# Gated product of 8192 x 8192 in fp32: four-row groups in three 64 KiB slots, products packed in place, stores of 64 KiB a partition

## The chip, the core and the metric

The kernel runs on one core of a Trainium2 chip. The core has a scalar engine (ACT), a vector engine (DVE), a sync engine (SP) that here only issues transfers, GpSimd (POOL), and 16 DMA engines that move data between the chip's memory (HBM) and the core's on-chip buffer (SBUF, 128 partitions). The metric is device time in microseconds (us), lower is better. Time before: 933.41 us, the median of three runs (933.37 to 933.46).

## The reference

The input is one fp32 matrix of 8192 rows and 8192 columns. The left half of each row is multiplied by the sigmoid of the right half:

```
def reference(x):
    a, b = np.split(x, 2, axis=-1)
    return a * (1 / (1 + np.exp(-b)))
```

So 268.4 MB are read, 134.2 MB are written, and each output element costs one sigmoid and one product.

## The kernel before

The rows are cut into 32 tiles of 256 rows. In a tile each of the 128 partitions holds two whole rows that follow each other in HBM: 64 KiB of input (`x_sb`, two slots) and 32 KiB of output (`o_sb`, two slots). A tile's input is one contiguous stretch of 8 MiB in HBM, its output one of 4 MiB.

For each tile `_tiles` records, in program order:

- L58, one load on SP's queue into the tile's input slot. It waits for the product that last read the slot, that is of two tiles before.
- L76, the sigmoid on ACT, in place over the right halves (one instruction of 128x8192 for both rows).
- L77, the product on DVE, from the input slot into the output slot.
- L70, one store on ACT's queue, which waits for the product.

The first tile and the last have four quarter instructions of 128x2048 instead of the one sigmoid and the one product, and the last tile's output goes out in four stores of 1 MiB, each when its quarter is done. The engines run their own instructions in order, and a DMA instruction that has to wait holds up what is behind it on its engine. The framework's automatic dependencies are reduced by hand (`implied`) to the ones that are needed.

L43 is a transfer that computes nothing. It goes out first on ACT's queue and reads 15 pieces of 64 bytes for each of 16 partitions into the tile `idle`, which nothing uses. Its packets stand in ACT's queue ahead of the first store's.

`_launch_early` moves the first load ahead of the start-up barrier, so that it is issued at time 0. `_close_on_sync` rewrites the closing: POOL waits for all transfers but the last and clears the semaphores, and SP waits for the last store. Both functions are left as they are.

A DMA is cut into one packet for each contiguous run of a partition: a load is 128 packets of 64 KiB, a store 128 packets of 32 KiB, so each of the 16 DMA engines gets 8 packets of it, and a 4-byte one that counts up the semaphore. Loads stand in SP's queue (q1 in the profile) and stores in ACT's (q10); the same 16 engines serve both.

Of the kernel before, what the change touches and what calls it, by code (L numbers as in the profile page):

```python
# [8 lines left out]
def _tiles(ctx, tc, x, out):  # L9

    nc = tc.nc
    P = nc.NUM_PARTITIONS  # L20
    DEP = mybir.DependencyInfo(mybir.DependencyClass.Sync, mybir.DependencyReason.DATA)
    fp32 = mybir.dt.float32
    SIG = mybir.ActivationFunctionType.Sigmoid

    n_rows, n_cols = x.shape
    half = n_cols // 2
    R = 2
    SLOTS = 2
    n_tiles = n_rows // (P * R)
    x_t = x.rearrange("(n p r) m -> n p (r m)", p=P, r=R)  # L30
    out_t = out.rearrange("(n p r) m -> n p (r m)", p=P, r=R)

    pool = ctx.enter_context(tc.tile_pool(name="io", bufs=1))
    xs = [pool.tile([P, R * n_cols], fp32, name=f"x_sb{k}") for k in range(SLOTS)]
    os = [pool.tile([P, R * half], fp32, name=f"o_sb{k}") for k in range(SLOTS)]

    def implied(later, *earlier):
        for e in earlier:
            tc.declare_no_dep(later.ins, e.ins, reason="follows from the waits that are kept")

    KEEP = 15
    idle = pool.tile([16, KEEP * 32], fp32, name="idle")
    held = nc.scalar.dma_start(  # L43
        out=idle.rearrange("p (k m) -> p k m", m=32)[:, :, 0:16],
        in_=x[0:16, 0 : KEEP * P].rearrange("p (k m) -> p k m", m=P)[:, :, 0:16],
    )
    tc.keep_in_program_order(held)

    gone = [{k: [] for k in ("loads", "sigs", "muls", "stores")} for _ in range(SLOTS)]
    last_stores = [[] for _ in range(SLOTS)]  # L50
    for i in range(n_tiles):
        old = gone[i % SLOTS]
        freed = last_stores[i % SLOTS]
        now = {k: [] for k in old}
        rows = xs[i % SLOTS].rearrange("p (r h m) -> p r h m", r=R, h=2)
        packed = os[i % SLOTS].rearrange("p (r m) -> p r m", r=R)

        load = nc.sync.dma_start(out=xs[i % SLOTS], in_=x_t[i])  # L58
        implied(load, *old["loads"], *old["sigs"])
        now["loads"].append(load)  # L60

        if 0 < i < n_tiles - 1:
            parts = [(slice(0, R), slice(0, half))]
        else:
            w = half // 2
            parts = [
                (slice(r, r + 1), slice(c * w, (c + 1) * w)) for r in range(R) for c in range(2)
            ]
        def store(cols):
            ins = nc.scalar.dma_start(out=out_t[i, :, cols], in_=os[i % SLOTS][:, cols])  # L70
            now["stores"].append(ins)

        chunks = []
        for k, (r, c) in enumerate(parts):
            b = rows[:, r, 1, c]
            sig = nc.scalar.activation(out=b, in_=b, func=SIG)  # L76
            mul = nc.vector.tensor_mul(out=packed[:, r, c], in0=rows[:, r, 0, c], in1=b)  # L77
            implied(sig, *old["sigs"], *old["muls"], *old["loads"])
            implied(mul, *old["muls"], *old["loads"], *now["loads"])
            by_sigmoid = i % 2 == 1 and len(parts) == 1  # L80
            implied(mul, *(s for s in old["stores"] if by_sigmoid or s not in freed))
            if by_sigmoid:
                for s in freed:
                    tc.add_manual_dep(sig.ins, s.ins.name, DEP, reason="frees the output slot")
            tc.keep_in_program_order(sig)
            now["sigs"].append(sig)
            now["muls"].append(mul)
            chunks.append(slice(r.start * half + c.start, r.start * half + c.stop))
            if i == n_tiles - 1 and k > 0:
                store(chunks[k - 1])  # L90
        store(chunks[-1] if i == n_tiles - 1 else slice(0, R * half))
        for s in now["stores"]:
            implied(s, *old["loads"], *old["sigs"], *old["muls"], *now["loads"], *now["sigs"])
        for k in old:
            old[k] += now[k]
        last_stores[i % SLOTS] = now["stores"]


def _launch_early(nc):
# [68 lines left out]
@with_exitstack  # L168
def kernel(
    ctx: ExitStack,  # L170
    tc: tile.TileContext,
    x: bass.AP,
    out: bass.AP,
):
    nc = tc.nc
    with ExitStack() as pools:
        _tiles(pools, tc, x, out)
    tc.close()
    tc.compile()
    _launch_early(nc)  # L180
    _close_on_sync(nc)
# [30 lines left out]
```

## Time and profile before

| | |
|---|---|
| median of the runs | 933.41 us |
| span of the profiled execution, first to last instruction | 931.87 us |
| median less span | 1.54 us |
| bytes moved | 402.68 MB, 432 GB/s over the span |
| DVE busy | 278.6 us (30%), 38 products |
| ACT busy | 227.0 us (24%), 38 sigmoids |
| sigmoid, 128x8192 and 128x2048 | 7029 and 1901 ns |
| product, 128x8192 and 128x2048 | 8692 and 2287 ns |
| load, issue to landing (median) | 42.2 us |
| store of 4 MiB, issue to landing (median) | 42.0 us |

The profile was taken from one execution. Its own time is the span of 931.87 us and what lies around it, which the runs put at 1.54 us. An engine's busy share says how much of the span it worked. The share of a DMA queue is the time that its packets took, over 16 engines and the whole span, so the shares of the queues add up to how busy the DMA engines were. The trace also has a record of every packet (queue, size, start, duration).

### The profile page before, as it was taken

How to read it: one execution, taken by the hardware profiler on the slowest of the kernel's cores; microseconds unless marked ns; L12 is line 12 of the kernel's file. 1: busy time of each engine (PE TensorE's matmuls, PEld its weight loads, DVE VectorE, ACT ScalarE, POOL GpSimd, SP SyncE). 2: the span in 40 equal slices, each digit the busy share in tenths (PEclk: the TensorE clock that was granted, in tenths of full speed). 3: DMA queues.
4: the chain of work that ended last, by engine and by line, in shares of the span. 5: the costliest groups of instructions: out<-in, count | busy, mean ns of one | idle time of the engine just before them, and what ended most of it. 6: DMA issues, size and time to landing. Idle time of an engine off the chain costs nothing.

```text
span 931.9 us, 249 instructions
## 1 busy us (share of the span) xinstructions
DVE 278.6 (30%) x38; ACT 227.0 (24%) x39; POOL 0.2 (0%) x4
## 2 busy tenths in 40 slices
DVE  0333312333123331133321333213332133321333
ACT  1413332133320333202332023320233202333023
POOL 0000000000000000000000000000000000000000
DMA  9999999999999999999999999999999999999999
GB/s 405 448 408 430 447 428 450 411 464 408 428 450 428 450 409 466 408 428 450 428 450 408 464 411 428 450 425 453 405 459 419 428 450 425 453 405 453 425 428 405
DMA packets 9905, 402.68 MB, mean 432 GB/s; under 512 B 1328, under 2 KB 1328, under 8 KB 1328
## 3 DMA queue, kind: packets, MB, share of 16 engines
q1 hardware_dynamic: 4608, 268.44, 66.6%
q10 hardware_dynamic: 5296, 134.24, 33.4%
q14 instruction: 1, 0.01, 0.0%
HBM read 268.45 MB, written 134.22 MB: 432 GB/s over the span
## 4 chain that ended last, share of the span: by engine, by line
DMA 72%; DVE 15%; ACT 12%; issue 0%; ACTq 0%
DMA x_sb<-in_x_dram 72%; DVE o_sb L77 15%; ACT x_sb L76 12%; ACTq L70 0%; ACTq L76 0%
## 5 line engine op out<-in xcount | busy, mean ns | idle before, releaser
L77 DVE TENSOR_TENSOR o_sb<-x_sb 128x8192 f32<-128x8192 f32 (+1 forms) x38 | 278.6, 7344 | 645.0 <-ACT x_sb L76 645.0
L76 ACT ACTIVATE x_sb<-x_sb 128x8192 f32<-128x8192 f32 (+1 forms) x38 | 225.7, 5950 | 693.2 <-DMA x_sb<-in_x_dram 691.9
L76 ACT ACT_TABLE_LOAD x1 | 1.3, 1283 | 1.2 <-PEq L196 1.2
L196 POOL MEMSET const-bfloat16-1.0<- 128x1 bf16 x1 | 0.1, 102 | 0.0
L196 POOL MEMSET const-uint8-127<- 128x1 uint8 x1 | 0.1, 101 | 0.0
L196 POOL MEMSET const-float32-0.0<- 128x1 f32 x1 | 0.1, 100 | 0.2 <-issue 0.2
L196 POOL MEMSET const-float32-1.0<- 128x1 f32 x1 | 0.1, 98 | 0.0
## 6 DMA issues: line engine op xcount, KB each, us to landing
out_dram<-o_sb ACTq DMA_DIRECT2D x31, 4096.0 KB, 42.0
out_dram<-o_sb ACTq DMA_DIRECT2D x4, 1024.0 KB, 7.9
x_sb<-in_x_dram SPq DMA_DIRECT2D x32, 42.2
idle<-in_x_dram ACTq DMA_DIRECT2D x1, 15.0 KB, 41.4
```

The source lines that it names most:

```text
L76: sig = nc.scalar.activation(out=b, in_=b, func=SIG)
L77: mul = nc.vector.tensor_mul(out=packed[:, r, c], in0=rows[:, r, 0, c], in1=b)
L196: nc = _bacc.Bacc("TRN2", target_bir_lowering=False, num_devices=1)
```

## The change

The tile becomes a group of 512 rows: each partition holds four rows that follow each other in HBM. A group has two halves of two rows, each loaded by one DMA of 8 MiB (L54 of the changed kernel), so that a partition's 64 KiB runs now lie 128 KiB apart in HBM. There are three slots of 64 KiB a partition and no output slots: the first half of a group goes to slot 0 or 2 in turn, the second half always to slot 1.

All sigmoids (L67) and products (L71) are half-row instructions of 128x2048, eight for each group. The products are packed in place: those of all four rows go, one behind the other, into the slot of the group's first half, over input that has been read. Three sigmoids of a group wait for the earlier product whose input lies where the following product will write: quarter 2 for product 0, quarter 3 for product 1, and the first of the second half for product 3.

A group's output goes out in one store of 64 KiB a partition, 8 MiB (L78). Exceptions: the first row of the first group is stored at once (16 KiB a partition) and its other three rows together (48 KiB); the last group goes out in two stores of 16 KiB a partition and four of 8 KiB.

The load of the next group's second half waits for the last product of this group, which frees slot 1. The load of the first half two groups on waits for this group's whole store to land, which frees its slot. Both stand on SP's queue in this order. The first load is cut in two (a row each, 32 KiB a partition), and the first four loads wait for nothing. The transfer into `idle` is gone.

There are 33 loads and 22 stores, where there were 32 loads, 35 stores and the transfer into `idle`. The core of the diff:

```
-    R = 2
-    SLOTS = 2
...
-    held = nc.scalar.dma_start(
-        out=idle.rearrange("p (k m) -> p k m", m=32)[:, :, 0:16],
-        in_=x[0:16, 0 : KEEP * P].rearrange("p (k m) -> p k m", m=P)[:, :, 0:16],
-    )
...
-        load = nc.sync.dma_start(out=xs[i % SLOTS], in_=x_t[i])
...
-            sig = nc.scalar.activation(out=b, in_=b, func=SIG)
-            mul = nc.vector.tensor_mul(out=packed[:, r, c], in0=rows[:, r, 0, c], in1=b)
...
+    R, H = 2, 2
+    n_groups = n_rows // (P * R * H)
+    x_t = x.rearrange("(g p h r) m -> g h p (r m)", p=P, h=H, r=R)
+    out_t = out.rearrange("(g p q) m -> g p (q m)", p=P, q=H * R)
+    slots = [pool.tile([P, R * n_cols], fp32, name=f"x_sb{k}") for k in range(3)]
+    def slot(g, h):
+        return 1 if h else 2 * (g % 2)
...
+    def load(g, h, needs=(), parts=1):
+        width = R * n_cols // parts
+        k = slot(g, h)
+        for j in range(parts):
+            c = slice(j * width, (j + 1) * width)
+            ins = place([k], nc.sync.dma_start(out=slots[k][:, c], in_=x_t[g, h][:, c]), *needs)
...
+    def work(g, h, k):
+        r, c = k // 2, k % 2 * quarter
+        of, to = slot(g, h), slot(g, 0)
+        a = slots[of][:, r * n_cols + c : r * n_cols + c + quarter]
+        b = slots[of][:, r * n_cols + half + c : r * n_cols + half + c + quarter]
+        at = (h * R + r) * half + c
+        before = {(0, 2): (g, 0, 0), (0, 3): (g, 0, 1), (1, 0): (g, 0, 3)}
+        over = [mul_of[m] for m in [before.get((h, k))] if m]
+        sig = nc.scalar.activation(out=b, in_=b, func=SIG)
+        place([of], sig, load_of[g, h, r], *over)
...
+        mul = nc.vector.tensor_mul(out=slots[to][:, at : at + quarter], in0=a, in1=b)
+        mul_of[g, h, k] = place(sorted({of, to}), mul, sig)
+    def store(g, lo, hi, done):
+        c = slice(lo * quarter, hi * quarter)
+        k = slot(g, 0)
+        ins = place([k], nc.scalar.dma_start(out=out_t[g][:, c], in_=slots[k][:, c]), done)
+        store_of.setdefault(g, []).append(ins)
+    load(0, 0, parts=2)
+    load(0, 1)
+    load(1, 0)
+    for g in range(n_groups):
+        first, final = g == 0, g == n_groups - 1
+        for k in range(4):
+            work(g, 0, k)
+            if first and k == 1:
+                store(g, 0, 2, mul_of[g, 0, 1])
+        if final:
+            store(g, 0, 2, mul_of[g, 0, 1])
+            store(g, 2, 4, mul_of[g, 0, 3])
+        for k in range(4):
+            work(g, 1, k)
+            if final and k > 0:
+                store(g, 3 + k, 4 + k, mul_of[g, 1, k - 1])
+        if final:
+            store(g, 7, 8, mul_of[g, 1, 3])
+            break
+        load(g + 1, 1, [mul_of[g, 1, 3]])
+        store(g, 2 if first else 0, 8, mul_of[g, 1, 3])
+        if g + 2 < n_groups:
+            load(g + 2, 0, store_of[g])
```

`place` keeps of the automatic dependencies only those that are named, and keeps the program order.

More of the change, by code (lines that the diff above doesn't have):

```diff
@@ L26, in _tiles @@
     half = n_cols // 2
-    R = 2
-    SLOTS = 2
-    n_tiles = n_rows // (P * R)
-    x_t = x.rearrange("(n p r) m -> n p (r m)", p=P, r=R)
-    out_t = out.rearrange("(n p r) m -> n p (r m)", p=P, r=R)
-    pool = ctx.enter_context(tc.tile_pool(name="io", bufs=1))
[L34 to L39, printed above, removed]
@@ L41, in _tiles @@
-    KEEP = 15
-    idle = pool.tile([16, KEEP * 32], fp32, name="idle")
-    held = nc.scalar.dma_start(
-        out=idle.rearrange("p (k m) -> p k m", m=32)[:, :, 0:16],
-        in_=x[0:16, 0 : KEEP * P].rearrange("p (k m) -> p k m", m=P)[:, :, 0:16],
-    )
[L47 to L96, printed above, removed]
@@ new lines, in _tiles @@
+    quarter = half // 2
+    R, H = 2, 2
+    n_groups = n_rows // (P * R * H)
+    x_t = x.rearrange("(g p h r) m -> g h p (r m)", p=P, h=H, r=R)
+    out_t = out.rearrange("(g p q) m -> g p (q m)", p=P, q=H * R)
+    pool = ctx.enter_context(tc.tile_pool(name="io", bufs=1))
+    slots = [pool.tile([P, R * n_cols], fp32, name=f"x_sb{k}") for k in range(3)]
+    traced = [[] for _ in slots]
+    load_of, mul_of, store_of = {}, {}, {}
+    def slot(g, h):
+        return 1 if h else 2 * (g % 2)
@@ new lines, in place @@
+    def place(touched, ins, *needs):
+        kept = {n.ins.name for n in needs}
+        seen = set()
+        for k in touched:
+            for e in traced[k]:
+                if e.ins.name not in kept | seen:
+                    seen.add(e.ins.name)
+                    tc.declare_no_dep(ins.ins, e.ins, reason="follows from the waits that are kept")
+            traced[k].append(ins)
+        tc.keep_in_program_order(ins)
+        return ins
+    def load(g, h, needs=(), parts=1):
[4 more added lines that the diff above has]
+            ins = place([k], nc.sync.dma_start(out=slots[k][:, c], in_=x_t[g, h][:, c]), *needs)
+            for r in range(R) if parts == 1 else [j]:
+                load_of[g, h, r] = ins
@@ new lines, in work @@
+    def work(g, h, k):
[8 more added lines that the diff above has]
+        place([of], sig, load_of[g, h, r], *over)
+        for m in over:
+            tc.add_manual_dep(sig.ins, m.ins.name, DEP, reason="read before the product goes over it")
+        mul = nc.vector.tensor_mul(out=slots[to][:, at : at + quarter], in0=a, in1=b)
+        mul_of[g, h, k] = place(sorted({of, to}), mul, sig)
```

## The prediction

> **What bounds the kernel now.** I read the page first: the slices, then the shares of the DMA queues.
>
> ```profile
> span 931.9 us, 249 instructions
> ...
> DVE 278.6 (30%) x38; ACT 227.0 (24%) x39; POOL 0.2 (0%) x4
> ...
> DMA  9999999999999999999999999999999999999999
> ...
> q1 hardware_dynamic: 4608, 268.44, 66.6%
> q10 hardware_dynamic: 5296, 134.24, 33.4%
> ```
>
> Loads (q1) and stores (q10) fill 66.6 + 33.4 = 100.0% of 16 DMA engines over the span. No slice is under 9. So the DMA engines set the end, and the chain of waits, which gives ACT and DVE 26%, misleads: its pieces lie beside transfers of other tiles. Next, the DMA view of one pair of tiles, 41.2 to 99.2 us:
>
> ```profile
> DMA packets 576, 25.17 MB, mean 434 GB/s; under 512 B 64, under 2 KB 64, under 8 KB 64
> ...
> q1 hardware_dynamic: 288, 16.78, 66.7%
> q10 hardware_dynamic: 288, 8.39, 33.5%
> ```
>
> Of 288 packets 256 carry data. A 64 KiB packet took 0.667 x 58 x 16 / 256 = 2.418 us, a 32 KiB one 0.335 x 58 x 16 / 256 = 1.215 us; the trace's packet records say 2.418 and 1.213. They alternate strictly, one load packet, one store packet, whatever their size. Two small packets cost 2 x 1.213 - 2.418 = 8 ns more than a large one, and neighbours in the records overlap by about 4 ns, so a packet costs 4 to 8 ns beside its bytes. Change of DMA costs two 4-byte records, 6 ns each: a tile takes 29.00 us, and 8 x (2.414 + 1.2097) = 28.99. **Time can go away only as packets, or as gaps of the DMA engines; it can come only as gaps or slower packets.** Gaps today: 1.0 us before the first packet, 0.6 us more in it, and one at 38 to 41 us. One engine's records there (start, queue and bytes, ns):
>
> ```
> 35.700 L65536 2453
> 38.149 S64 11
> 38.156 L65536 3095
> 41.248 S4 9
> 41.254 L4 9
> 41.260 S32768 1213
> ```
>
> The load packet took 3.095 us in place of 2.45, and so on all 16 engines: 0.65 us at the first store's start, behind the transfer into `idle`.
>
> **The change, part by part.**
>
> *Packets.* For each DMA engine: before 256 load and 248 + 32 store packets = 536. After: loads 31 x 8 + 2 x 8 = 264, stores 22 x 8 = 176, together 440. 96 fewer, at 4 to 8 ns: -0.4 to -0.8, I take -0.5 us (nearer to the period of 29.00, which holds the 4). DMAs with their 4-byte packet: 68 to 55, 13 x 6 ns = -0.1 us.
>
> *The transfer into `idle`.* 15 packets of 11 ns (about 7 after the overlap) = -0.1 us, and six load packets beside them that took 2.453 instead of 2.418: -0.2 us. The gap of 0.65 us: it goes if it belongs to this transfer's end, and stays if it belongs to the first store as such. I take it as gone, because a ring that wakes up in the middle of load packets cost nothing in the one other place (the first 64-byte packet at 6.50 stands behind a load packet of 2.418). Ends 0 and -0.65.
>
> *Sigmoids and products.* After, 128 of 128x2048 each: ACT 128 x 1.9 = 243 us, DVE 128 x 2.285 = 292 us, 14 more than now. All of it lies beside transfers: eight products are 18.3 us of a group's 24 x 2.414 = 57.94. Costed at nothing while the loads queued are enough to cover it; what it costs otherwise is rival 1. In place or in another tile, I give a product the same time; no row shows the difference.
>
> *Waits.* The wait for products 0, 1 and 3 holds sigmoids 2 and 3 of a first half by some 0.5 us and 0.1 us; behind them stand only sigmoids that are not late. Dangerous are the two loads on SP. Count from B, the end of a group's last load packet. Landing to ACT: 1.08 us (41.25 to 42.33). Four sigmoids and products:
>
> ```profile
> 22.03 7.31 ACT L76 ACTIVATE x_sb<-x_sb 128x2048 f32<-128x2048 f32 x4 [19.54 <-DMA x_sb<-in_x_dram]
> 23.97 8.89 DVE L77 TENSOR_TENSOR o_sb<-x_sb 128x2048 f32<-128x2048 f32 x4 [23.97 <-ACT x_sb L76]
> 32.89 25.55 SPq L58 DMA_DIRECT2D x_sb<-in_x_dram  x2
> 32.90 0.37 ACTq L70 DMA_DIRECT2D out_dram<-o_sb  x1
> ```
>
> These lines are before's first tile: the sigmoids' start at 22.03, the end of the products at 23.97 + 8.89 = 32.86, both issues at once. So store and next load are issued at B + 1.08 + 10.83 + 0.03 = B + 11.95. Issue to first packet: 1.0 to 1.6 us on empty queues (the first load), at most 4.1 under way (the store issued at 916.86 follows at 920.93 without a gap). I take 1.3: ready at B + 13.25. Meanwhile the other half-group's load runs in packets of 2.414. When the transfer into `idle` was issued, at 0.78, the packet running and one more came first; so here packet 6 and packet 7, and the store starts at 7 x 2.414 = B + 16.90. Eight alternations, 1:1 now: its last packet ends at 16.90 + 15 x 2.414 = B + 53.11, lands 0.83 later (70.25 to 71.08 for before's first store), and the load that waits for it on SP is ready at 53.11 + 0.83 + 0.05 + 1.3 = B + 55.3. The loads queued by then last until 24 x 2.414 = B + 57.94. **Margin 2.6 us, no gap.** Nothing else stands behind that load on SP. ACT waits for the store's product with the next group's sigmoids behind, whose load lands at about B + 23: late for nobody.
>
> *Ends.* At the start 24 MiB of loads are queued without a wait (58 us of transfers), and the first row's store goes in between: they last until 1.6 + 24 x 2.414 + 8 x 0.606 = 64.4, and the first group's last product is due at 45.1 + 11.95 = 57.1. At the end the store packets left when the loads stop last 14 x 0.606 = 8.5 us, and the first quarter's store is ready at 1.08 + 1.91 + 2.29 + 1.3 = 6.6; further quarters come every 2.2 us, each with 8 x 0.306 = 2.45 us of packets. No gap, as now (912 to 931: store packets all the way).
>
> *Sum.* -0.5 - 0.1 - 0.3 - 0.65 = -1.55 us against the execution's 931.87 + 1.54 = 933.41, which is also the median. **931.9 us**; with the gap at the first store 932.5, with the packets at 8 ns and all gone 931.5.
>
> **Two rules of the Trainium skill, weighed.** The trace shows loads whose runs lie 64 KiB apart at 2.418 us a packet, and no run at 128 KiB. "DMA: Bandwidth & Descriptors", section "Latency and other measured facts", tells of copies that lose with the run's pitch: at 512 KiB 207 GB/s of 214 that are full, at 2 MiB 164. By its 3%, which it gives for four times this pitch, the loads' 619 us would grow by an estimated 20 us; below that pitch it has no row, and I add nothing. The trace shows the change from one DMA to the next at 12 ns. [...]
>
> **Rivals.**
>
> 1. *The load queue runs dry once in a group: slower.* The load two groups on waits for the whole 8 MiB store, where before it waited for a product. For it: the margin is one packet. If issue to first packet takes over 14.48 - 11.95 = 2.5 us in mid-stream (the rows allow 1.0 to 4.1), the store slips by a packet, its last one ends at B + 55.52, at 2.6 us the load is ready at 55.52 + 0.88 + 2.6 = 59.0, 1.07 us late, and each gap also costs 0.6 us of refilling, as in the first packet. A gap makes the next group earlier against its loads, so every second group has one: 7 x (1.07 + 0.6) = 11.7 us at 2.6, 7 x (2.57 + 0.6) = 22 at 4.1, and then smaller gaps in the other groups too. 943 to 959, most likely 944. Against: the first load's 1.0 to 1.6.
> 2. *Each waking of the store queue costs the 0.65 us seen at 41 us: slower.* Before, stores stand in q10 without a break; now it is empty for 57.94 - 36.2 = 22 us in each group. 15 x 0.65 = 9.8 us: 941.6. Against: the waking at 6.50.
> 3. *Reads at 128 KiB pitch are slower.* Each 1% on a load packet is 6.2 us; below, nothing to gain, as the load packets ran at one speed throughout. No bound from a row above; at 1 to 2% 938 to 944.
> 4. *The stores' 64 KiB runs go out as two packets of 32 KiB*: 120 packets come back, +0.6: 932.5, no change.
>
> **How the numbers follow.** Forecast 0.65, its own range 931.4 to 932.8; rival 1 0.20; rival 2 0.07; rival 3 0.06; rival 4 0.02. A measurement of this kernel tells 0.2% (1.9 us) from no change, so faster begins under 931.5: only the forecast with every term at its good end, and something more at the start or end, 0.12. Within 0.2%: 0.53 + 0.02 = 0.55. Slower: 0.33. The range takes in the forecast, rivals 2 and 4, and the nearer halves of rivals 1 and 3: 931.3 to 945.0, which leaves out some 0.16 (rival 1 above 945 about 0.09, rival 3 0.02, below 931.3 0.05).
>
> **What would show it.** Right: both DMA queues' shares add up to 100% again; 4224 data packets in q1 and 2816 in q10, 2.418 us at 64 KiB for both; a period of 57.94 us from group to group; the load two groups on issued about 2.6 us plus 1.3 before its first packet; no long packet at the first store. Rival 1: DMA slices under 9 at 58 or 116 us steps, a store that starts at B + 19.3. Rival 2: one load packet of about 3.1 us at each store's start. Rival 3: load packets over 2.43 us throughout. The forecast is wrong if the sum of the shares falls under 99.5%.

## The result and the profile after

The changed kernel takes **947.58 us** (median; 945.78 to 951.10), the kernel before 933.39 us in the same comparison: a ratio of **1.0156, 95% interval 1.0144 to 1.0168**. The forecast was 931.9, with a range of 931.3 to 945.0. The profiled execution took 945.78 us, its span is 944.4 us, 12.5 more than before's 931.87. The page of after:

```profile
span 944.4 us, 374 instructions
...
DVE 284.9 (30%) x128; ACT 238.8 (25%) x129; POOL 0.2 (0%) x4
...
DMA  9999999999999999999999999999999999999998
...
q1 hardware_dynamic: 4752, 268.44, 66.8%
q10 hardware_dynamic: 3168, 134.22, 32.8%
q14 instruction: 2, 0.02, 0.0%
```

The packets are the forecast ones: 4752 less 528 of 4 bytes are 4224 in q1, 3168 less 352 are 2816 in q10. The DMA row is full and the shares still add up to 99.6%. So by the page alone nothing seems lost, and yet the same bytes took 12.5 us longer. A share counts the time that a packet is under way, and a packet that stalls in the middle counts as busy. What shows the loss is the rate. Stretches of 58 us (columns: stretch, its length, busy time of DVE, ACT and POOL, clock, DMA share, GB/s), before:

```profile
110.00:168.00 58.00, 17.41 (x3) 14.06 (x2) 0.00 (x0) 1.00 1.00 434
...
748.00:806.00 58.00, 17.39 (x3) 14.06 (x2) 0.00 (x0) 1.00 1.00 434
```

and after:

```profile
110.00:168.00 58.00, 17.68 (x9) 14.84 (x8) 0.00 (x0) 1.00 1.00 434
...
342.00:400.00 58.00, 16.58 (x8) 14.84 (x8) 0.00 (x0) 1.00 1.00 432
400.00:458.00 58.00, 17.06 (x9) 14.65 (x8) 0.00 (x0) 1.00 1.00 417
458.00:516.00 58.00, 15.24 (x8) 12.29 (x8) 0.00 (x0) 1.00 1.00 428
516.00:574.00 58.00, 17.24 (x8) 14.29 (x9) 0.00 (x0) 1.00 0.99 421
...
748.00:806.00 58.00, 17.80 (x8) 13.76 (x8) 0.00 (x0) 1.00 1.01 424
```

At first after runs at before's 434 GB/s, up to 400 us at 432; then it falls to between 417 and 428 with the share still at about 1.00. The issues of the stores say the same: 110.94, 169.06, 227.14, 285.20 (58.06 to 58.12 apart), then 58.6 to 60.5 apart.

How the packets lie is seen in the DMA view of two such stretches, each cut into 40 slices of 1.45 us; a packet's bytes count where it starts. First 110 to 168 us, then 748 to 806 us of after:

```profile
GB/s 226 497 723 0 723 226 497 723 0 723 226 497 723 0 723 271 452 723 0 723 271 452 723 0 723 316 407 723 0 723 316 407 723 0 723 316 407 723 0 723
```

```profile
GB/s 633 226 588 316 407 633 226 588 271 362 90 588 316 542 316 407 588 316 542 316 407 588 316 542 316 407 588 316 542 316 407 588 316 542 316 407 588 316 452 407
```

In the first stretch the 16 DMA engines go in step: in some slices all of them start a packet (723), and in every fifth none does (0). In the second there is no empty slice left: some engines stand a part of a packet or a whole one behind the others. I call the time between the first and the last engine at the same packet their **spread**. Before, it is 0.5 to 0.7 us from end to end; in after, at the last packet of each store, it is 0.4 at the start, 1.5 at 325 us and 2 to 4 from 380 us on.

In the packet records the loss can be summed up, as time over the usual length of a packet (2.418 us at 64 KiB), mean of 16 engines: load packets lose 11.8 us in after (before 1.5, all in the first 42 us), store packets 0.1, idle time is 4.4 us (before 1.7). That is 10.3 + 2.7 more, and less the 0.5 us of packets saved the 12.5 us of the spans. Of the 11.8 us 9.5 lie in one kind of load: the first half of a group, which waits for a whole store. (The records do not name the engine. Where a reading below goes by engine, I chained them by start and end; between engines that stand a whole packet apart this can swap two.)

### The profile page after: what moved, and what is told of

It is laid out like the page before. It is cut to its first block, busy times and chain, and to the rows that moved or that the text cites. A ratio compares the mean times of both kernels' runs of the same rounds, so it can differ in the third digit from the quotient of the medians.

```text
span 944.4 us, 374 instructions
## 1 busy us (share of the span) xinstructions
DVE 284.9 (30%) x128; ACT 238.8 (25%) x129; POOL 0.2 (0%) x4
## 3 DMA queue, kind: packets, MB, share of 16 engines
q1 hardware_dynamic: 4752, 268.44, 66.8%
q10 hardware_dynamic: 3168, 134.22, 32.8%
## 4 chain that ended last, share of the span: by engine, by line
DMA 81%; DVE 15%; ACT 3%; issue 0%; ACTq 0%; SPq 0%
DMA x_sb<-in_x_dram 81%; DVE x_sb L71 15%; ACT x_sb L67 3%; ACTq L78 0%; SPq L54 0%; ACTq L67 0%
## 5 line engine op out<-in xcount | busy, mean ns | idle before, releaser
L71 DVE TENSOR_TENSOR x_sb<-x_sb 128x2048 f32<-128x2048 f32 x128 | 284.9, 2287 | 652.3 <-ACT x_sb L67 652.3
L67 ACT ACTIVATE x_sb<-x_sb 128x2048 f32<-128x2048 f32 x128 | 237.5, 1901 | 695.3 <-DMA x_sb<-in_x_dram 681.3
```

Of the source, the lines that this page charges most:

```text
L71: mul = nc.vector.tensor_mul(out=slots[to][:, at : at + quarter], in0=a, in1=b)
```

## The experiments

The theories have letters, where an expectation does not say itself what one stands for. Where only one time is given, the kernel ran once. A and B put the loss on the loads by themselves (A on the 128 KiB from run to run), G on each waking of the store queue (a store that starts after the queue was empty), D on the thin margin of the load that waits for a store, D' on an instruction fetch that makes a DMA engine late, E on 64 KiB store packets beside 64 KiB load packets by themselves, D2 on the wait of a load for the whole store, with engines that stand apart.

### Loads and their pitch

**e1**: after, with each load's rows in one stretch (64 KiB from run to run).

```
-    x_t = x.rearrange("(g p h r) m -> g h p (r m)", p=P, h=H, r=R)
+    x_t = x.rearrange("(g h p r) m -> g h p (r m)", p=P, h=H, r=R)
```

> The changed kernel with one edit: each load reads one contiguous 8 MiB again, so a partition's 64 KiB runs lie 64 KiB apart instead of 128 KiB; slots, waits, packets and stores are those of the changed kernel. (The rows then reach the output in another order than the reference's; the work is the same.) Theory A, the load packets are slow because of the 128 KiB pitch, in the stretches where loads run alone: 931.9 to 932.6 us, load packets back at 2.418 us. Theory B, load packets are slow wherever loads run alone in the middle of the run, whatever their pitch: 945 to 951 us as for the changed kernel. Theory C, the waking of the store queue costs it: 945 us too, with the long packets only at the stores' starts.

Measured: 944.38 us (941.38 to 948.15), ratio 1.0131 (1.0096 to 1.0166). The loss stays, and starts at the same place.

**e2**: before, with after's pitch.

```
-    x_t = x.rearrange("(n p r) m -> n p (r m)", p=P, r=R)
+    x_t = x.rearrange("(g p h r) m -> g h p (r m)", p=P, h=2, r=R)
...
-        load = nc.sync.dma_start(out=xs[i % SLOTS], in_=x_t[i])
+        load = nc.sync.dma_start(out=xs[i % SLOTS], in_=x_t[i // 2, i % 2])
```

> The kernel before with one edit: the loads' runs lie 128 KiB apart (rows again reach the output in another order), nothing else. Here a load packet always alternates with a store packet, except in the first 41 us. Theory A as I hold it (the pitch hurts where loads run alone at 434 GB/s of reads): only the first 41 us and nothing or little after, 933.4 to 935 us. A stronger theory A (the pitch hurts everywhere): 3% on the load packets, 945 us or more. Theories B and C: 933.4 us.

Measured: 933.25 us (933.20 to 933.39), ratio 0.9999 (0.9990 to 1.0008). **r1** and **r2** make the 32 loads alone, at either pitch, and one store at the end:

```
+    for i in range(n_groups * H):
+        nc.sync.dma_start(out=xs[i % 3], in_=x_t[i // H, i % H])
+    nc.scalar.dma_start(out=out_t[0], in_=xs[i % 3][:, 0 : R * half])
```

> Loads alone: the 32 loads of 8 MiB into three slots in turn and one store at the end; no sigmoid, no product, no other store (left out). Runs 64 KiB apart. 256 packets of 2.414 us for each DMA engine are 618 us, some 622 with the start and the end. Theory A: 622 us. Theory B: the same 3% as in the lone stretches of the changed kernel (10.4 us in some 350), 635 us or more.

> Loads alone as in the run with 64 KiB, but runs 128 KiB apart. Theory A: 635 us or more, with load packets of 2.5 us and over in the mean. Theory B: the same time as with 64 KiB, both slow. Theory C: 622 us, no slow packets, as no store starts.

Measured: 636.28 and 636.27 us; the loads end at 622.09 us in both, and the last store, which I had left out of the sum, takes the rest. No long load packet after the first. Pages of r1 and r2:

```profile
span 634.5 us, 79 instructions
...
q1 hardware_dynamic: 4608, 268.44, 97.8%
```

```profile
span 634.5 us, 79 instructions
...
q1 hardware_dynamic: 4608, 268.44, 97.9%
```

The span and the time of a packet are the same at both pitches, so A and B fall. The Trainium skill, "DMA: Bandwidth & Descriptors", section "Latency and other measured facts", has a loss at 512 KiB of pitch and more, in copies between tensors in HBM; at the 128 KiB of these loads the ratio of 0.9999 shows none.

### Wakings, the transfer into `idle`, the fetch

**e6**: before without L41 to L48, the transfer into `idle`.

> The kernel before without the transfer into idle, nothing else. The sum of the prediction gave -0.3 us for its packets and -0.65 us for the gap at the first store. The changed kernel has no such transfer and still shows a gap of 0.7 us at its second store, so I now expect the gap to stay: 933.0 us. If the gap was the transfer's: 932.4 us. If the transfer keeps the store queue behind the loads, so that the last tile's products are covered by store packets: a gap at the end, 935 us or more.

Measured: 933.19 us against 933.40, ratio 0.9998 (0.9989 to 1.0007). The long load packet at the first store is still there (0.88 to 1.11 us over). It belongs to the first store, and after has it too (0.26 us at 21 us and 0.70 at 57).

**g0** runs before with quarter instructions for all tiles, as a base; **g2** and **g4** are g0 with only every second or every fourth tile stored:

```
-        if 0 < i < n_tiles - 1:
+        if False:
...
-        store(chunks[-1] if i == n_tiles - 1 else slice(0, R * half))
+        if i % 2 == 0 or i == n_tiles - 1:
+            store(chunks[-1] if i == n_tiles - 1 else slice(0, R * half))
```

> Control for the next two: the kernel before with every tile in quarter instructions on ACT and DVE (as the first and the last tile are), stores and loads as they were. ACT has as many sigmoids as the changed kernel and should fetch instructions at some 350 us too. Theory D' (a fetch in the middle starts the trouble in any schedule): long load packets after it, 938 us or more. Theory G (trouble needs a store queue that runs empty and wakes up beside loads alone): 933.4 us, nothing after the fetch.

> As the control, but only every second tile (and the last) is stored; the other outputs are left out. Store packets stay 32 KiB, no load waits for a store, and a load's margin is 19.3 - 13.3 = 6 us, so the load queue cannot run dry by a wait. Store packets alternate with loads half of the time, then the loads run alone for 19 us and the next store wakes the queue, 15 times. Clean sum for a DMA engine: 256 x 2.414 + 128 x 1.21 + 32 x 0.306 = 782.6, with start, end and the 1.5 us outside some 788 us. Theory D (the trouble is the load that waits for a store): 788 us. Theory G (each waking can cost 0.3 to 1.8 us, as seen in the changed kernel after 336 us): 795 us or more, long load packets just ahead of the stores' first packets.

> As the last one with every fourth tile stored: 7 to 8 wakings, each after loads alone for some 58 us. Clean sum 256 x 2.414 + 64 x 1.21 + 32 x 0.306 = 705.2, some 710.5 us in all. Theory D: 710.5 us. Theory G: 714 us or more, with as much or more for each waking as with every second store.

Measured: g0 933.87, g2 788.52, g4 711.62 us, the two latter 0.5 and 1.1 over their clean sums of 788 and 710.5. After the first store a waking costs 0.00 to 0.01 us, so a waking by itself costs nothing, and G falls. In g0 the fetch of ACT's instructions, at 289 and 366 us, put one engine back and cost nothing.

**e3a** and **e3b** move that fetch (after has it at 336.4 and 338.9 us): the first half of a group in row instructions, or its quarters in four pieces.

```
-        mul = nc.vector.tensor_mul(out=slots[to][:, at : at + quarter], in0=a, in1=b)
+        mul = nc.vector.tensor_mul(out=slots[to][:, at : at + n], in0=a, in1=b)
...
+        cut = 4 if h == 0 else 1
+        for j in range(cut):
+            p = slice(j * w, (j + 1) * w)
```

> The changed kernel with the first half of each group in two row instructions (128x4096) in place of four quarters on ACT and DVE; the second half, on which the store waits, is left. ACT has some 9 instructions a group instead of 11, so its 63rd, where the fetch came at 336 us, falls at some 400 us. Theory D: the schedule is clean until then, the long load packets start after the fetch, 938 to 948 us. Theory E: they start at about 336 us as before.

> The changed kernel with the first half's quarters cut into four pieces of 128x512 each on ACT and DVE: 16 instructions in place of four, in time that is not on the path. ACT reaches its 63rd instruction in the third group. Theory D: the fetch comes at 130 to 180 us, and further fetches follow; long load packets from then on, 945 to 960 us. Theory E: they start at about 336 us.

Measured: 958.59 and 948.60 us. In e3a the fetch comes at 462 us, but the engines split at the very first store and the loss begins at 99 us; in e3b fetches come from 119 us on and the loss begins at 215. e3a is slower than D had it, and neither loss starts at 336 us, as E had it. The fetch is one thing that moves engines apart, and not needed. D' falls.

### The wait of a load for a store

**e5** widens the margin, by 5 us on paper: the second half is loaded by rows, each as soon as its row is free.

```
-            ins = place([k], nc.sync.dma_start(out=slots[k][:, c], in_=x_t[g, h][:, c]), *needs)
+            ins = place([k], nc.sync.dma_start(out=slots[k][:, c], in_=x_t[g, h][:, c]), *(needs if parts == 1 else needs[j : j + 1]))
...
-        load(g + 1, 1, [mul_of[g, 1, 3]])
+        load(g + 1, 1, [mul_of[g, 1, 1], mul_of[g, 1, 3]], parts=2)
```

> The changed kernel, but the load of a group's second half is two DMAs, one row each (32 KiB packets), each waiting for the products that read its row. The stores stay one of 64 KiB a partition, the first half's load still waits for the whole store. The last two quarters alone are left to do when the last load packet lands: the store is issued at B + 1.08 + 6.44 = B + 7.5 instead of B + 11.95, so it ends two packets earlier and the margin of the load behind it grows from 2.6 to some 7.5 us. Theory D (the margin of one packet is used up when one DMA engine falls behind, first by the fetch of ACT's instructions at 336 us; from then the load queues of the others run dry in each group): 932.3 to 933.5 us, some 0.6 of it for 8 more packets a group, and no long load packets after 336 us. Theory E (64 KiB stores alternating 1:1 with loads drive the engines apart by themselves): 940 us or more.

Measured: 949.48 us (946.17 to 955.03), ratio 1.0172 (1.0125 to 1.0219). No better, so a thin margin is not the whole cause. The loss has another form: the spread at the stores' last packets grows to 3 to 7 us, one engine is late at a time, load packets lose 7.7 us and store packets as much (in after 0.1), and 4.9 of the 6.3 us of idle time lie at the end. The loads that wait for a store lose at most 0.5 us each.

**e4** makes two stores of 32 KiB a partition out of each store; the slot's next load waits for both.

```
-            store(g, 2, 4, mul_of[g, 0, 3])
+        store(g, 2 if first or final else 0, 4, mul_of[g, 0, 3])
...
-        store(g, 2 if first else 0, 8, mul_of[g, 1, 3])
+        store(g, 4, 8, mul_of[g, 1, 3])
```

> The changed kernel, but a group's output goes out in two stores of 32 KiB a partition, the first as soon as the first half's products are done; the slot's next load waits for both. The second store then has 4 MiB: it starts at B + 16.9, its last packet ends 8 x 3.62 - 2.41 later, at B + 43.5, and the margin of the load behind it is some 12 us. Theory D: 932.8 to 933.5 us (the packets of the kernel before, without the transfer into idle), no long load packets. Theory E: the same. Theory F (any load that waits for a store's landing costs a gap in each group): 940 us or more.

Measured: 934.63 us (934.50 to 934.82), ratio 1.0014 (1.0004 to 1.0023). Stretches of e4:

```profile
110.00:168.00 58.00, 10.92 (x6) 11.07 (x6) 0.00 (x0) 1.00 1.00 433
...
400.00:458.00 58.00, 17.82 (x9) 14.86 (x9) 0.00 (x0) 1.00 1.00 434
...
748.00:806.00 58.00, 17.74 (x9) 14.79 (x9) 0.00 (x0) 1.00 1.00 434
```

The loss is gone, but two things have changed: the packet, and the margin. A store lands earlier against the load that waits for it. I count this **reserve** from the end of the store's last packet on the slowest engine to the end of the queued loads on the fastest: 12.05 us in e4, in every group from the second on, and 6.7 in after as long as its engines go in step. In e4 the queue ran dry once, behind the first group's stores at 99 us (reserve -1.56); its engines stand 1.8 us apart from then on and lose nothing.

**h1** and **h3** take the wait alone. Both leave the products in place in two input slots and store from a third tile that is never written again:

```
     def slot(g, h):
-        return 1 if h else 2 * (g % 2)
+        return h
...
-        k = slot(g, 0)
-        ins = place([k], nc.scalar.dma_start(out=out_t[g][:, c], in_=slots[k][:, c]), done)
+        k = 2
+        ins = place([k], nc.scalar.dma_start(out=out_t[g][:, c], in_=slots[k][:, c]), *traced[2][:1])
+        tc.add_manual_dep(ins.ins, done.ins.name, DEP, reason="stored when the product is done")
...
+            load(g + 1, 0, [mul_of[g, 0, 3]])
```

h3 adds after's wait to that load:

```
+            for m in store_of.get(g - 1, []):
+                tc.add_manual_dep(load_of[g + 1, 0, 0].ins, m.ins.name, DEP, reason="as in the changed kernel")
```

> After's sigmoids, products and store issues at the same points, but no load waits for a store: the products stay in place in two 64 KiB input slots, each load waits only for the product that last read its slot, as in the kernel before, and the stores (64 KiB a partition, one for each group, same sizes at start and end as in after) are taken from a third tile that is filled once with a constant. So the output is left out. The bytes, the packets and the wakings of the store queue are after's, only the wait of a load for a store is gone. Theory E (64 KiB store packets that alternate with 64 KiB load packets make the DMA engines slower by themselves): 943 to 950 us, with long load packets at the stores' starts in most groups. Theory D2 (it is the load that waits for the whole store: it starts on a dry queue or on engines that stand a packet apart, and this carries on to the next group): 931.5 to 934 us, no long load packet behind the first store.

> The same kernel with one wait put back: the load of a group's first half also waits until the store of two groups before has landed, as in after. The output is left out as before. Nothing else differs, and by after's schedule the wait ends 2.6 us before the load is needed. D2: slow as after, 941 to 950 us, with the gaps at the loads that wait. E: the same as without the wait, within 2 us.

Measured: h3 947.68 us (946.00 to 950.56), ratio 1.0162 (1.0136 to 1.0188), which is after's. h1 took 938.02 (the profiled execution), 984.78, 934.47 and 968.66 us, so no one time and no interval stands for it: its two shorter executions lie below all four of h3, its two longer ones above, and those two have no trace. Stretches of the profiled h1 and of h3:

```profile
400.00:458.00 58.00, 17.80 (x9) 14.62 (x8) 0.00 (x0) 1.00 1.00 434
458.00:516.00 58.00, 17.73 (x9) 14.62 (x8) 0.00 (x0) 1.00 1.00 434
516.00:574.00 58.00, 17.88 (x9) 14.62 (x8) 0.00 (x0) 1.00 1.00 433
748.00:806.00 58.00, 16.93 (x9) 13.97 (x8) 0.00 (x0) 1.00 1.00 431
```

```profile
400.00:458.00 58.00, 17.03 (x9) 14.62 (x8) 0.00 (x0) 1.00 1.01 434
458.00:516.00 58.00, 16.67 (x9) 13.94 (x8) 0.00 (x0) 1.00 0.99 417
516.00:574.00 58.00, 16.21 (x8) 13.03 (x8) 0.00 (x0) 1.00 0.99 415
748.00:806.00 58.00, 17.80 (x8) 13.53 (x9) 0.00 (x0) 1.00 1.00 424
```

h1's engines are no better in step than h3's, yet it keeps 431 to 434 GB/s where h3 falls to 415 to 424. It isn't clean either: its profiled span is 936.6 us, 4.8 over before's. The packet records show where the difference lies. Groups of after and, for the same load, of h1; times in us, ranges over the 16 engines; the last column is the time lost in the load that comes next:

```
        store's last packet ends  queued loads end  reserve  lost
after   149.87..150.40            157.12..157.65    6.72     0.02
        323.79..325.27            331.04..332.52    5.77     0.15
        381.74..384.48            389.16..391.47    4.68     1.08
        441.00..444.84            448.00..450.45    3.16     1.68
        736.65..739.69            744.06..746.70    4.38     1.81
h1      324.23..327.60            331.47..333.48    3.87     0.04
        498.27..501.45            505.51..507.58    4.06     0.02
        847.65..850.42            853.94..856.26    3.51     0.03
```

Over the five kernels with after's wait (after, e1, e3a, e3b, h3; 70 groups): a reserve under 4.5 us costs 1.67 us on average (1.11 to 2.30, 31 groups), one over 5.2 us 0.07 (at most 0.36, 28 groups), between them 0 to 1.8. (The ends are taken from the 16 packets that end last. By the 4-byte packets, one for each engine, the earliest end comes up to 0.2 us sooner; then 33 groups lie under 4.5 us and cost 1.63.) In h1 the load does not wait for the store, and with a reserve of 3.5 to 4.8 us, in ten groups, it loses 0.01 to 0.04. So **the wait, met by engines that stand apart, is shown to go with most of after's loss**: 9.5 of its 12.5 us lie in the loads that wait, and the same loads lose next to nothing when the wait is left out. It ends with the slowest engine, and on the engines that are ahead the load queue has by then run dry or down to its last packet. The Trainium skill, "DMA: Bandwidth & Descriptors", section "Why a DMA increments its semaphore by 16 and not by 1", states that the engines of a DMA finish independently and only the full count says that all has landed; the group at 441 us agrees, with last packets that end 3.84 us apart and a load issued only behind the last. SP's queue there, in the timeline of after:

```profile
447.63 0.33 SPq L54 DMA_DIRECT2D x_sb<-in_x_dram  x1
```

The fastest engine's queue ended at 448.00, 0.37 us later. The next load's first packet began at 448.59.

But the dry queue is only the smaller part of the price. Of the 62.1 us that these loads lose in the five kernels, the first two of an engine's eight packets (by order of start) have 14.7 and the last two 45.0; in after it is 3.7 and 5.2 of 9.5. The last two run 15 to 20 us after the wait has ended, just ahead of the next store's first packet. One engine of after, behind the store that ends at 384.48 us, start in us, queue and bytes, ns:

```
401.304 L65536 2418
403.718 L65536 2441
406.156 L65536 3660
409.812 S65536 2418
```

On all 16 engines the load packet ahead of the store took 2.9 to 4.1 us there. In the 5 us ahead of a store's first packet, from the second group's store on, load packets lose 5.5 us in all of after (0.04 at most at each store up to 348 us, up to 1.43 from 407 us on), 10.0 in h3, and 0.15 in h1, which wakes its store queue just as often. So this part, too, goes with the wait; how a wait that came late makes packets long so much later, no run shows.

**h2** has loads and 64 KiB stores 1:1 without a waking and without the wait: h1 with 16 loads and a store after each.

```
         if g + 2 < n_groups:
+            load(q + 1, h, [mul_of[q, h, 3]])
+        store(g, 0, 8, mul_of[q, h, 3])
```

> Only the first 16 loads of 8 MiB are made, and after each a store of 8 MiB from the constant tile, so loads and stores of 64 KiB a packet alternate 1:1 all the time and the store queue does not run empty. Half of the input and the output are left out. Clean sum for a DMA engine: 256 packets of 2.414 us are 618 us, and some 1.6 us ahead of the first packet, 0 to 14 us without a packet ahead of the last store and 2 us at its end: 622 to 636 us. E: each load packet's mean over 2.45 us in mid-run, 630 to 650 us. D2: mean 2.42 us, long packets only at the first store.

Measured: 636.55 us, 0.55 over the clean sum's upper end. Long packets are not the rule: 12 of the 16 engines have none after the first store. But the engine that is last drifts from 0.7 us behind the first at 44 us to 7.1 at 314 us, while the first loses nothing (a steady 38.64 us from load to load); from then until 553 us the distance stays at 7.1 to 7.2, three whole packets.

### Wide margins

**h4** and **h5** are h1 and h3 without sigmoids and products, so that loads and stores are issued 10.8 us earlier.

```
-            load(g + 1, 0, [mul_of[g, 0, 3]])
+            load(g + 1, 0, [load_of[g, 0, 0], load_of[g, 0, 1]])
...
-        store(g, 2 if first else 0, 8, mul_of[g, 1, 3])
+        store(g, 2 if first else 0, 8, load_of[g, 1, 1])
```

> The kernel h1 (no load waits for a store, stores from a constant tile) without sigmoids and products: a load waits only for the landing of the load that last filled its slot, a store for the landing of its group's second half. Computation and output are left out; DMAs, packets and wakings of the store queue are those of after. By after's rows a load is then ready 1.08 + 0.05 + 1.3 = 2.4 us after a landing, and the other slot's load lasts at least 8 x 2.414 = 19.3 us: a margin of some 17 us in place of 6. If the time is lost because a wait ends after the last of 16 DMA engines that stand up to 7 us apart (D2 with the engines' spread as its size): 931 to 934 us in every run. If 64 KiB store packets beside 64 KiB load packets are slow by themselves (E): erratic as h1, 935 us and up to 985.

> The same, with after's wait put back: the load of a group's first half waits for the landing of the store of two groups before. Without the 10.8 us of sigmoids and products the store is issued at B + 1.1, its last packet ends at about B + 41, and the load is ready at B + 43.2, 14.7 us before it is needed in place of 2.6. Computation and output are left out. D2 with the spread as its size: 931 to 934 us, as the wait is over in time on every engine. If a load that waits for a store is slow whatever the margin: 941 to 950 us.

Measured: 944.23 us (942.76 to 946.36), ratio 1.0123 (1.0107 to 1.0140), and 942.95 (942.79 to 943.82), ratio 1.0104 (1.0089 to 1.0119). Both are above D2's 931 to 934. h5 lies in the band of a load that is slow whatever the margin, but h4, which has no such wait, is no faster, so that isn't it either. Stretches of h5 (here the columns are DVE, POOL, clock, DMA share, GB/s):

```profile
110.00:168.00 58.00, 0.00 (x0) 0.00 (x0) 1.00 1.00 434
...
516.00:574.00 58.00, 0.00 (x0) 0.00 (x0) 1.00 1.00 432
748.00:806.00 58.00, 0.00 (x0) 0.00 (x0) 1.00 1.00 431
```

The gaps at the load that waits are gone: h5's reserve is 7.3 to 16.3 us (by the 4-byte packets), and the first packets of that load are not long (at most 2.44 us). Load packets lose 5.1 us where h3 lost 13.7. But the spread is still there, up to 9.7 us at 853 us, and is paid at the end: 6.5 of h5's 7.7 us of idle time come after 870 us, when the stores that are left wait for the last engine's last load. Between 116 and 696 us about half of the engines have no long packet; the others lose up to 1.6 us in a stretch of 58 us.

**h6** is h5 with each 64 KiB store as two of 32 KiB.

```
-        store(g, 2 if first else 0, 8, load_of[g, 1, 1])
+        store(g, 2 if first else 0, 4, load_of[g, 1, 1])
+        store(g, 4, 8, load_of[g, 1, 1])
```

> The kernel h5 (DMAs alone, a load waits for the store of two groups before, wide margins) with each 64 KiB store issued as two of 32 KiB a partition, one behind the other; nothing else differs, and computation and output are left out as there. A load packet alternates with half as large a store packet, so the stores of a group last 16 x 3.62 = 58 us and the store queue no longer runs empty. If it is the 64 KiB store packet that lets the DMA engines drift apart, and the drift that costs h5 its 9.5 us: 932 to 934 us, engines less than 3 us apart all the way, no long load packets behind the start. If these bare kernels are slow for another reason: 941 to 945 us as h5.

Measured: 955.43 us (950.96 to 957.79), ratio 1.0225 (1.0192 to 1.0258). Half of the expectation held: the engines start the loads within 0.9 us of each other for 540 us. The other half was a mistake in my schedule: 16 store packets at 3.62 us end after the 16 load packets beside them, so the wait is too late by construction. The reserve is -3.1 to -4.8 us in every second group and over 9 in the others. Two stretches of h6, without and with such a group:

```profile
229.00:287.00 58.00, 0.00 (x0) 0.00 (x0) 1.00 0.98 425
287.00:347.00 60.00, 0.00 (x0) 0.00 (x0) 1.00 1.00 419
```

This is rival 1 in its pure form: engines in step, a dry load queue in every second group, 23 us of span in seven groups. It does not tell the packet size from the rest. So D2 stands for what after loses at the load that waits, and not for all that the kernels with 64 KiB stores lose: e5, h4 and h5, with a wider margin or without the wait, still take 942.95 to 949.48 us. That after without a late wait would be fast isn't shown.

## Why the prediction was wrong

**What bounds it, and the packets: right.** The DMA engines set the end, a 64 KiB store packet stays one packet of 2.418 us (so rival 4 falls), and loads and stores alternate 1:1. The group's last load packet ends at 99.16 to 99.56 on the 16 engines and the store issued at 110.94 starts at 116.06 to 116.46, which is B + 16.90 as forecast. Up to 340 us the order of packets is the forecast one but for one turn (below). The period was to be 57.94 and was 58.06 to 58.12 there, before's being 58.00. The 0.5 us of saved packets, 0.04 in a group, are too small to be seen in it; they fit the sum of the spans above.

**The gap at the first store: wrong.** The term of -0.65 us was given to the transfer into `idle`. e6 shows that the gap stays without it, and e6 as a whole that the transfer costs nothing that can be measured (0.9998).

**Sigmoids and products: right.** They cost nothing by themselves: 58 us stretches at 434 GB/s with eight of each, in g0 as well.

**The waits, "Margin 2.6 us, no gap": this is the step that failed.** The landing was nearly right: on the first engine (B = 99.16) the load was to be issued at B + 54.0 = 153.15 and was at 153.28. Nor was the 1.3 us from issue to first packet too short: where the fastest queue had run dry, the first packet came 0.95 to 1.09 us after the issue (448.59 after 447.63 in after). What was wrong is the margin made of them. First, the count was made for one DMA engine as if it were 16. The landing is that of the slowest, the dry queue that of the fastest, and their spread comes off the margin in full. At 0.5 us the margin held, which is why 340 us went as forecast; at 2 to 4 us it was gone. Second, a load that arrives just in time isn't free. By the 70 groups a load loses nothing only when the reserve is about 5.2 us; SP issues some 2.75 us into it, so 2.45 us must be left at the issue. Of the 3.84 us that were there at 153.28, 1.4 were free, not 2.6. Why it takes 2.45 us is open.

**Rival 1: the right place and, by luck, the right price; a wrong trigger.** It said 943 to 959 us and 1.07 + 0.6 = 1.7 us a gap; measured are 947.58 and 1.67. But its price was worked out for a gap and the refilling at the load's start, where only about a quarter of the loss lies in the five kernels. No store slipped by a packet at B + 16.90, and the gaps do not come in every second group: they come where the reserve is under 5 us, in after in six of the last nine groups that have such a wait. It had a chance of 0.20, and the range took in only its nearer half, up to 945. With a margin of one packet, its whole band belonged in the range.

**Rival 2: its sign came, its cause did not.** One load packet of about 3.1 us at each store's start was its mark, and from 407 us on after shows such packets, of up to 4.1 us: 5.5 us in all, where it had 9.8. But a waking by itself costs 0.00 to 0.01 us in g2 and g4, and h1, with after's wakings and 64 KiB stores, loses 0.15 us there in all. **Rival 3** falls by e1, e2, r1 and r2.

**The test was blind.** The forecast was to be wrong if the shares fell under 99.5% in sum. They came to 99.6%, since a stalled packet counts as busy.

**What stays open.** Why the engines move apart is not settled, nor why a late load makes packets long at the next store. All kernels with 64 KiB store packets did it (after, e1, e3a, e3b, e5, h1 to h5: 2 to 10 us), those with 32 KiB or with loads alone stayed within 1.3 us (before, e2, e6, g0, g2, g4, r1, r2; in e4 once 1.8 us behind a dry queue, in h6 up to 2.4 us late in the run). That is a coincidence in the runs and no mechanism; a kernel that changes the packet size alone, with a wide margin on both sides, was not run. Nor is it known what h1 lost in its two long executions, of which there is no trace. And none of these kernels is faster than before by an amount that can be measured: without a reserve to spare nothing was won, and with it, in e4, 1.2 us were lost.

## What to carry to other kernels

Where a load waits for a store, or any DMA for another, count the margin from the slowest DMA engine's last packet to the fastest engine's empty queue; here a load was free of loss from about 5 us on, and lost 1.67 us under 4.5. A margin of one packet on paper, counted on one engine, was none. A wide reserve alone did not bring the time back in h5 (7.3 to 16.3 us), so look at the engines' spread as well. A full DMA row and shares of 100% do not say that nothing is lost: compare GB/s stretch by stretch with a stretch that is known to be clean. When a change makes the schedule tighter for a gain of under 0.2%, as here, the range belongs to the rival that breaks it.

## What the runs showed of the hardware

- **The 4-byte packet that ends a DMA takes a turn of its own.** One engine of after, start in us, queue and bytes, ns:

```
147.558 S65536 2418
149.973 L65536 2418
152.387 S4 9
152.393 L65536 2418
```

  The store's data ended at 149.976, its count only at 152.396, behind a whole load packet. In the same way a load's 4-byte packet takes a turn and lets two store packets stand together (120.977 and 123.397), which ended the store's data one packet early. In my count the two errors cancelled to 0.1 us.
- **A late engine can be made later.** In h2 the last engine fell back by 6.4 us between 44 and 314 us and 12 of the 16 engines had no long packet there, although all do the same work.
- **A spread can stay and cost nothing.** In e4 it is 1.8 to 1.9 us on the loads from 104 to 888 us, beside a reserve of 12.05 us. In h5, with 64 KiB stores, it grew beside a reserve of 7.3 to 16.3 us, and was paid at the end.
- **The first store costs once.** In before, after, e6 and g0 load packets lose 0.8 to 1.1 us around the first two stores; later wakings of the store queue cost 0.00 to 0.01 us by themselves (g2, g4).
- **A transfer issued on a queue that has run dry starts its first packet about 1 us later**: 0.95 to 1.09 us in ten groups of after, e1, e3a and e3b.
